# Two-layer hybrid decoder trunk: GpSimd takes 37 of the 258 weight-chunk subtractions, and the order of work is planned again

## The chip, the cores and the metric

The kernel runs on one core of one Trainium2 chip. A core has a TensorE (PE in the profile), a VectorE (DVE), a ScalarE (ACT), a GpSimd (POOL) and a SyncE (SP, which issues nearly all DMAs). The metric is the device time of one execution in microseconds. The kernel before takes 805.81 us, the median of three runs (805.7 to 805.99).

## The reference, cut to what matters

```python
for l in range(DEPTH):                       # 2 layers, x is 256 x 1024, float32
    h = rms_norm(x, g_mix[l])
    q_a, k_a, v_a, u_b, cq_c, ckv_c, kpe_c, gate_logits = split(h @ w_in[l])   # 1024 x 5280
    y_a = swa_attention(q_a, k_a, v_a, ...)        # 8 heads, window 128
    y_b = conformer_conv(u_b, w_dw[l], ...)        # GLU, depthwise conv of width 31, LayerNorm, swish
    y_c = mla_attention(cq_c, ckv_c, kpe_c, ...)   # low-rank query / key-value, 8 heads, causal
    branches = einsum([y_a, y_b, y_c], w_branch[l])
    x = x + (sigmoid(gate_logits) * branches).sum(branch) @ w_out[l]
    x = x + square(relu(rms_norm(x, g_mlp[l]) @ w_up[l])) @ w_down[l]   # 1024 -> 4096 -> 1024
return rms_norm(x, g_final)
```

Every weight is used once, and all is float32.

## The kernel before, in words

**Chunks.** The weights come through as 258 chunks of 128 x 1024 float32, 129 per layer, numbered i = 0 to 257 in the order of use: glu 8, kv 4, q 4, lr 2, up 3, gate 24, branch 12, out 8, mu 32 (the up projection of the MLP) and md 32 (its down projection). So layer 0 has kv0 as chunks 8 to 11, q0 as 12 to 15 and gate0 as 21 to 44; layer 1 has glu1 as 129 to 136, kv1 as 137 to 140, q1 as 141 to 144 and gate1 as 150 to 173.

**The split.** PE multiplies in a rounded 32-bit form (F32R). To keep float32's accuracy every chunk is split in two: `chunk()` loads it by DMA into a tile `raw` (5 buffers), ScalarE rounds it into `whi` (4 buffers), and VectorE subtracts, `wlo = raw - whi` (4 buffers). Each product is then three matmuls: high by high, high by low, low by high. `wlo` holds what the title of such a change calls the following bits. In the gate stage (`token_major`) a chunk is 12 matmuls of 512 columns, 4 of them with `wlo`.

**Other work of VectorE.** The depthwise convolution (`conv`) is 124 instructions per layer, each a multiply-add over 128 x 256 that reads `u` and `acc` in SBUF; it is spread between the splits of the kv, q and gate stages, and its result is needed at the last third of the branch stage. The softmax of both attentions, the evacuations of the accumulators in PSUM and the MLP's squares are VectorE's and ScalarE's too. GpSimd has 54 instructions: constants, a few statistics of two or four numbers a row, and one scaling of a 128 x 1024 tile (`gf`).

**The order of work.** Nothing is issued as the program is read. `Engine` records each operation with an estimated cost in a `Plan`; `Plan.place` then plays the whole program through as a list scheduler and writes the order of every engine's queue, which the chip follows as it stands. An operation's rank is the chunk number plus or minus an entry of the table `K`: `split_gate0` is how many chunks ahead gate0's splits rank, `conv_0` and `conv_end0` are where the convolution's first and last step rank. Among ready operations an engine takes the one that can start first, with a small allowance (`PATIENCE`) for a better-ranked one that comes a little later. `LATENCY` says how long after an operation on one engine its reader on another may start. So VectorE's queue is a fixed sequence: if one of its instructions is late, all behind it are.

All instructions carry one line of the helper that issues them (L407), so rows are told apart by tile names.

Of the kernel before, what the change touches and what calls it, by code (L numbers as in the profile page):

```python
# [16 lines left out]
ALU = mybir.AluOpType  # L17
# [40 lines left out]
for l in range(DEPTH):  # L58
# [2 lines left out]
    K.update({f"{s}{l}": v[l] for s, v in PLACE.items()})  # L61

K.update({
# [9 lines left out]
})  # L73

PATIENCE = {"PE": 0.0, "ACT": 0.001, "DVE": 0.006, "POOL": 0.0, "DMA": 0.0}

FLOOR = {"rope": 12.0, "dist": 20.0, "squares": 9.5}

# [126 lines left out]
class Op:  # L205
# [13 lines left out]
    "PE": {"PE": 0.0, "ACT": 0.2, "DVE": 0.2, "POOL": 0.2, "DMA": 0.2},  # L219
    "ACT": {"PE": 0.27, "ACT": 0.12, "DVE": 0.13, "POOL": 0.15, "DMA": 0.15},  # L220
    "DVE": {"PE": 0.25, "ACT": 0.13, "DVE": 0.13, "POOL": 0.16, "DMA": 0.15},
    "POOL": {"PE": 0.2, "ACT": 0.1, "DVE": 0.06, "POOL": 0.1, "DMA": 0.1},
    "DMA": {"PE": 2.3, "ACT": 2.3, "DVE": 2.3, "POOL": 2.3, "DMA": 2.3},
}

# [1 line left out]
class Plan:  # L227
# [68 lines left out]
    def place(self):  # L296
# [21 lines left out]
        while True:  # L318
            best = None
            for e, ops in avail.items():  # L320
                now, mine = clock[e], None
                for op in ops:
# [10 lines left out]
                    else:  # L333
                        c = (t + PATIENCE[e] * op.rank, op.rank, rank[op], t)
                        if mine is None or c < mine[0]:
# [144 lines left out]
def trunk(ctx: ExitStack, tc: tile.TileContext, A, out):  # L480
# [9 lines left out]
    T, V, SC = Engine(plan, "PE", nc.tensor), Engine(plan, "DVE", nc.vector), Engine(plan, "ACT", nc.scalar)  # L490
    G, Q = Engine(plan, "POOL", nc.gpsimd), Engine(plan, "DMA", nc.sync)
# [284 lines left out]
    used, section = [0], [""]  # L776
# [4 lines left out]
    def chunk(rotary=False):  # L781


        i = used[0]
        used[0] += 1
        with plan.at(i - 20.0):
            raw = plan.tile([P, 1024], F32, "raw")
            loads[i](raw)
        with plan.at(Key(i, **{"split_" + section[0]: -1}) if i else Key(-12)):
            hi, lo = plan.tile([P, 1024], F32R, "whi"), plan.tile([P, 1024], F32R, "wlo")  # L790
            cuts = () if rotary else ((0, 512), (512, 1024)) if i == 0 else ((0, 1024),)
            for c0, c1 in cuts:
                a, b, c = (v[:, c0:c1] for v in (raw, hi, lo))
                SC.copy(out=b, in_=a)
                V.tensor_tensor(out=c, in0=a, in1=b, op=ALU.subtract)
            if rotary:
                a, b, c = (v.rearrange("p (k c) -> p k c", c=256) for v in (raw, hi, lo))
                SC.copy(out=b[:, :, 0:192], in_=a[:, :, 0:192])
                V.tensor_tensor(out=c[:, :, 0:P], in0=a[:, :, 0:P], in1=b[:, :, 0:P], op=ALU.subtract)
                V.tensor_tensor(out=b[:, :, 192:256], in0=a[:, :, P:192], in1=b[:, :, P:192], op=ALU.subtract)  # L800
        plan.key = Key(i)
        return hi, lo
# [26 lines left out]
    def feature_major(xh, xl):  # L829

        banks = [bank("mm"), bank("mm")]
        for k in range(4):
            hi, lo = chunk()
            for ct in range(4):
                o = banks[ct // 2][:, (ct % 2) * 256:(ct % 2 + 1) * 256]
                for kk in range(2):
                    kt = 2 * k + kk
                    cs = slice(kk * 512 + ct * P, kk * 512 + (ct + 1) * P)
                    mm3(o, hi[:, cs], lo[:, cs], xh[kt // 4][:, kt % 4, :], xl[kt // 4][:, kt % 4, :],
                        kt == 0 and ct % 2 == 0, kt == 7 and ct % 2 == 1)  # L840
        return banks

    def feature_pairs(xp):


        banks = [bank(t) for t in ("mm", "mm", "ps", "ps")]
        for k in range(4):
            hi, lo = chunk()


            cts = [(ct,) for ct in range(4)] if k == 3 else [range(4)]
            for some in cts:
                for short in (False, True):
                    for ct in some:
                        for kk in range(2):
                            kt = 2 * k + kk
                            cs = slice(kk * 512 + ct * P, kk * 512 + (ct + 1) * P)
                            both = xp[kt // 4][:, kt % 4, :, :]
                            if short:
                                T.matmul(out=banks[ct][:, 0:S], lhsT=lo[:, cs], rhs=both[:, 0, :], start=False, stop=kt == 7)  # L860
                            else:
                                T.matmul(out=banks[ct], lhsT=hi[:, cs], rhs=both.rearrange("p a s -> p (a s)"), start=kt == 0,
                                         stop=False)
        return banks

    def token_major(banks, nchunk, kt0, ah, al, first, last):

        for k in range(nchunk):
            hi, lo = chunk()
            for t in range(2):  # L870
                for kk in range(2):
                    kt = kt0 + 2 * k + kk
                    ts = slice(t * P, (t + 1) * P)
                    cs = slice(kk * 512, (kk + 1) * 512)
                    mm3(banks[t], ah[kt // 4][:, kt % 4, ts], al[kt // 4][:, kt % 4, ts], hi[:, cs], lo[:, cs],
                        first and k == 0 and kk == 0, last and k == nchunk - 1 and kk == 1)
# [279 lines left out]
    for l in range(DEPTH):  # L1156
# [16 lines left out]
        for g in range(2):  # L1173
            bk = feature_major(xh, xl)
            with evacuation():
                gate, a = plan.tile([P, 512], F32, "p"), plan.tile([P, 512], F32, "pT")
# [255 lines left out]
```

## Time and profile before

| | |
|---|---|
| median of 3 runs | 805.81 us (805.7 to 805.99) |
| the profiled execution | 805.54 us, its span 803.8 us |
| PE busy | 789.3 us, 98% |
| DVE busy | 616.4 us, 77%, 982 instructions |
| ACT busy | 468.7 us, 58% |
| POOL busy | 23.9 us, 3%, 54 instructions |
| chain that ended last | PE 94% |

How to read it: busy is the time with an instruction in the engine; a matmul's end is modelled and overlaps the next, so the start-to-start distance of matmuls tells the pace. The last instruction of the program ends 803.8 us after the first; 1.7 us lie around that span. In the rows below a timeline row gives start, duration, engine, operation, output<-inputs with shapes, and in brackets the idle time of the engine before it with what ended it.

### The profile page before, as it was taken

How to read it: one execution, taken by the hardware profiler on the slowest of the kernel's cores; microseconds unless marked ns; L12 is line 12 of the kernel's file. 1: busy time of each engine (PE TensorE's matmuls, PEld its weight loads, DVE VectorE, ACT ScalarE, POOL GpSimd, SP SyncE). 2: the span in 40 equal slices, each digit the busy share in tenths (PEclk: the TensorE clock that was granted, in tenths of full speed). 3: DMA queues.
4: the chain of work that ended last, by engine and by line, in shares of the span. 5: the costliest groups of instructions: out<-in, count | busy, mean ns of one | idle time of the engine just before them, and what ended most of it. 6: DMA issues, size and time to landing. Idle time of an engine off the chain costs nothing.

```text
span 803.8 us, 12447 instructions
## 1 busy us (share of the span) xinstructions
PE 789.3 (98%) x4613; PEld 677.0 (84%) x4613; DVE 616.4 (77%) x982; ACT 468.7 (58%) x778; POOL 23.9 (3%) x54
## 2 busy tenths in 40 slices
PE   8999999999999999999999999999999999999996
PEld 6998888888888888888899978888888888888885
DVE  6999999979867887545469999888896778764543
ACT  7666875756555556435354599755646555653442
POOL 2200000000000000000000000000000000010000
PEclk9999999999999999999999999999999999999998
DMA  8697456534666665666667634366466666665641
GB/s 287 177 208 215 129 157 167 174 110 161 205 184 191 191 185 190 184 193 186 196 184 165 163 107 131 107 194 198 133 208 185 189 192 186 191 210 188 203 133 52
DMA packets 124044, 140.85 MB, mean 175 GB/s; under 512 B 51792, under 2 KB 68560, under 8 KB 123984
## 3 DMA queue, kind: packets, MB, share of 16 engines
q1 hardware_dynamic: 123280, 139.51, 59.0%
q8 instruction: 36, 0.59, 0.3%
q10 hardware_dynamic: 704, 0.56, 0.2%
q14 instruction: 24, 0.20, 0.1%
HBM read 138.93 MB, written 1.11 MB: 174 GB/s over the span
## 4 chain that ended last, share of the span: by engine, by line
PE 94%; ACT 1%; DVE 1%; DMA 1%; issue 1%; SPq 0%; POOL 0%; POOLq 0%; ACTq 0%; DVEq 0%
PE bank_mm L407 73%; PE bank_ps L407 17%; PE bank_yb L407 3%; PE bank_tp L407 1%; DMA raw<-in_w_in 1%; ACT p L407 1%; DVE wlo L407 0%; SPq L407 0%; ACT whi L407 0%; POOL rstd L407 0%; DVE rope L407 0%; ACT junk L407 0%; ACT x L407 0%; DVE kpe L407 0%; POOL s L407 0%
## 5 line engine op out<-in xcount | busy, mean ns | idle before, releaser
L407 DVE TENSOR_TENSOR wlo<-raw,whi 128x1024 fp32r<-128x1024 f32 (+1 forms) x259 | 313.4, 1212 | 146.9 <-ACT whi L407 144.9
L407 ACT CAST whi<-raw 128x1024 fp32r<-128x1024 f32 (+1 forms) x259 | 270.1, 1045 | 260.7 <-PE bank_mm L407 173.0
L407 PE MATMUL bank_mm<-xp,whi 128*128 128x256 f32 (+1 forms) x832 | 177.8, 320 | 0.4 <-DVE p L407 0.4
L407 PEld LDWEIGHTS bank_mm<-xp,whi 128*128 128x128 f32 x832 | 131.6, 191 | 5.3 <-PE bank_mm L407 0.6
L407 PE MATMUL bank_mm<-whi,xp 128*128 128x512 f32 x384 | 128.4, 400 | 0.2
L407 PE MATMUL bank_mm<-xp,wlo 128*128 128x256 f32 x528 | 120.3, 282 | 0.4 <-DVE wlo L407 0.4
L407 DVE SCALAR_TENSOR_TENSOR acc<-u,wdw,acc 128x256 f32<-128x256 f32 x240 | 101.8, 477 | 0.0
L407 PEld LDWEIGHTS bank_mm<-xp,wlo 128*128 128x128 f32 x528 | 93.6, 190 | 7.5 <-DVE wlo L407 0.8
L407 PE MATMUL bank_mm<-whi,fh 128*128 128x512 f32 x256 | 99.8, 390 | 0.0
L407 PE MATMUL bank_mm<-wlo,fh 128*128 128x512 f32 x256 | 99.6, 389 | 0.0
L407 PE MATMUL bank_mm<-whi,fl 128*128 128x512 f32 x256 | 99.6, 389 | 0.0
L407 PEld LDWEIGHTS bank_mm<-whi,xp 128*128 128x128 f32 x384 | 72.1, 188 | 17.0 <-issue 1.2
L407 PE MATMUL bank_mm<-wlo,xp 128*128 128x512 f32 x192 | 75.3, 392 | 2.1 <-DVE wlo L407 1.9
L407 PE MATMUL bank_ps<-xp,whi 128*128 128x512 f32 x256 | 71.9, 392 | 0.0
L407 PEld LDWEIGHTS bank_mm<-whi,fl 128*128 128x128 f32 x256 | 48.1, 188 | 9.9
L407 PEld LDWEIGHTS bank_mm<-wlo,fh 128*128 128x128 f32 x256 | 48.1, 188 | 9.9
L407 PEld LDWEIGHTS bank_mm<-whi,fh 128*128 128x128 f32 x256 | 48.1, 188 | 9.8
L407 PEld LDWEIGHTS bank_ps<-xp,whi 128*128 128x128 f32 x256 | 45.7, 188 | 7.9
L407 PEld LDWEIGHTS bank_mm<-wlo,xp 128*128 128x128 f32 x192 | 36.2, 188 | 9.5 <-DVE wlo L407 3.0
L407 PE MATMUL bank_ps<-xp,wlo 128*128 128x256 f32 x256 | 43.4, 282 | 0.0
L407 PEld LDWEIGHTS bank_ps<-xp,wlo 128*128 128x128 f32 x256 | 38.5, 191 | 2.8
L407 ACT ACTIVATE p<-p,rinv 128x128 f32<-128x128 f32 (+1 forms) x64 | 25.1, 453 | 1.5 <-DVE rinv L407 1.5
(214 smaller groups left out, 971.5 us busy)
## 6 DMA issues: line engine op xcount, KB each, us to landing
raw<-in_w_up SPq DMA_DIRECT2D x64, 512.0 KB, 3.9
raw<-in_w_down SPq DMA_DIRECT2D x64, 512.0 KB, 3.7
raw<-in_w_in SPq DMA_DIRECT2D x48, 512.0 KB, 3.6
raw<-in_w_in SPq DMA_DIRECT2D x48, 256.0 KB, 3.3
raw<-in_w_branch SPq DMA_DIRECT2D x24, 512.0 KB, 3.6
raw<-in_w_out SPq DMA_DIRECT2D x16, 512.0 KB, 4.0
raw<-in_w_in SPq DMA_DIRECT2D x32, 128.0 KB, 2.9
spread<-far SPq DMA_DIRECT2D x16, 128.0 KB, 3.8
```

Of the source, the lines that this page charges most:

```text
L407: return fn(**real)
```

## The change

In the seven stages named in a new table `SHARE`, a chunk whose number leaves the remainder 1 by 2 has its subtraction issued on GpSimd and not on VectorE. For the stages that are not in the table the divisor is 1 << 20, and chunk 1 (in glu0) leaves the remainder 1 by that as well. So it is 4 chunks of glu1 (129, 131, 133, 135), 2 each of kv0 (9, 11), kv1 (137, 139), q0 (13, 15) and q1 (141, 143), 12 each of gate0 (21 to 43) and gate1 (151 to 173), and chunk 1: 37 in all. Each is one `tensor_tensor` of 128 x 1024. The planner's latency from GpSimd to PE goes from 0.2 to 1.4, and the table `K`, and with it the order of all queues, is another one. `cost_pool`, which the planner uses, is as it was.

```diff
 K.update({
-    "bias": 3, "dist": -10, "small": 6, "rope": -23, "split_glu0": 21, "split_kv0": 17, "split_q0": 8, "split_lr0": -9,
-    "split_up0": 4, "split_gate0": 17, "split_branch0": -7, "split_out0": -41, "split_mu0": 10, "split_md0": 19,
+    "bias": -2, "dist": -5, "small": 6, "rope": -26, "split_glu0": 26, "split_kv0": -10, "split_q0": 16, "split_lr0": -6,
+    "split_up0": 24, "split_gate0": 23, "split_branch0": -13, "split_out0": -42, "split_mu0": 8, "split_md0": 18,
...
-    "conv_0": 41, "conv_end0": 55, "ln_0": 35, "split_glu1": 21, "split_kv1": 28, "split_q1": 20, "split_lr1": -15,
-    "split_up1": -21, "split_gate1": 23, "split_branch1": 10, "split_out1": -15, "split_mu1": -11, "split_md1": 24,
+    "conv_0": 28, "conv_end0": 91, "ln_0": 35, "split_glu1": 44, "split_kv1": 41, "split_q1": 28, "split_lr1": -17,
+    "split_up1": -5, "split_gate1": 27, "split_branch1": 18, "split_out1": 2, "split_mu1": -13, "split_md1": 9,
...
-    "conv_1": 24, "conv_end1": 150, "ln_1": 10,
+    "conv_1": 40, "conv_end1": 117, "ln_1": 2,
 })
 
 PATIENCE = {"PE": 0.0, "ACT": 0.001, "DVE": 0.006, "POOL": 0.0, "DMA": 0.0}
+
+SHARE = {"glu1": 2, "kv0": 2, "kv1": 2, "q0": 2, "q1": 2, "gate0": 2, "gate1": 2}
...
-    "POOL": {"PE": 0.2, "ACT": 0.1, "DVE": 0.06, "POOL": 0.1, "DMA": 0.1},
+    "POOL": {"PE": 1.4, "ACT": 0.1, "DVE": 0.06, "POOL": 0.1, "DMA": 0.1},
...
                 SC.copy(out=b, in_=a)
-                V.tensor_tensor(out=c, in0=a, in1=b, op=ALU.subtract)
+
+                (G if i % SHARE.get(section[0], 1 << 20) == 1 else V).tensor_tensor(out=c, in0=a, in1=b, op=ALU.subtract)
```

## Rows read from the trace of the kernel before

**Rows 1.** The page: busy time by engine, and the granted clock in 40 slices.
```profile
PE 789.3 (98%) x4613; PEld 677.0 (84%) x4613; DVE 616.4 (77%) x982; ACT 468.7 (58%) x778; POOL 23.9 (3%) x54
PEclk9999999999999999999999999999999999999998
```

**Rows 2.** Who waited for whom: us in total, times, longest.
```profile
ACT whi L407 <- PE bank_mm L407: 173.0, 113, 2.6
...
PE bank_mm L407 <- DVE wlo L407: 2.4, 4, 1.2
```

**Rows 3.** Timeline of PE where it waits for a low part.
```profile
73.20 0.50 PE L407 MATMUL bank_mm<-wlo,xp 128*128 128x512 f32 x1 [0.76 <-DVE wlo L407]
...
463.24 0.50 PE L407 MATMUL bank_mm<-wlo,xp 128*128 128x512 f32 x1 [1.18 <-DVE wlo L407]
```

**Rows 4.** Busy time by stretch: length, then PE, PEld, DVE, ACT, POOL, clock, DMA.
```profile
66.00:92.00 26.00, 25.13 (x191) 21.69 (x188) 25.33 (x64) 22.68 (x64) 1.77 (x4) 1.00 0.55 170
...
104.00:168.00 64.00, 64.00 (x344) 51.98 (x342) 61.83 (x120) 42.62 (x77) 0.00 (x0) 1.00 0.56 167
...
401.00:420.00 19.00, 19.00 (x139) 17.99 (x138) 11.49 (x16) 10.20 (x17) 1.49 (x5) 1.00 0.59 178
420.00:449.00 29.00, 29.00 (x245) 29.00 (x244) 27.67 (x50) 13.14 (x18) 0.00 (x0) 1.00 0.82 172
...
490.00:519.00 29.00, 29.00 (x187) 22.94 (x186) 25.84 (x57) 26.41 (x68) 0.00 (x0) 1.00 0.43 120
519.00:568.00 49.00, 49.00 (x223) 40.67 (x222) 40.91 (x65) 24.80 (x27) 0.69 (x1) 1.00 0.61 183
```

**Rows 5.** Timeline of ACT, DVE and PE around chunk 37 of gate0.
```profile
129.77 1.06 ACT L407 CAST whi<-raw 128x1024 fp32r<-128x1024 f32 x1 [1.08 <-PE bank_mm L407]
...
130.87 1.22 DVE L407 TENSOR_TENSOR wlo<-raw,whi 128x1024 fp32r<-128x1024 f32 x1
132.00 1.67 DVE L407 SCALAR_TENSOR_TENSOR acc<-u,wdw,acc 128x256 f32<-128x256 f32 x4
133.59 1.22 DVE L407 TENSOR_TENSOR wlo<-raw,whi 128x1024 fp32r<-128x1024 f32 x1
...
129.12 0.39 PE L407 MATMUL bank_mm<-wlo,xp 128*128 128x512 f32 x1
...
129.80 0.39 PE L407 MATMUL bank_mm<-wlo,xp 128*128 128x512 f32 x1
...
130.48 0.39 PE L407 MATMUL bank_mm<-wlo,xp 128*128 128x512 f32 x1
```

**Rows 6.** Busy time by stretch, the convolution's steps (tile acc) on DVE alone.
```profile
104.00:168.00 64.00, 37.21 (x89) 1.00 0.56 167
```

**Rows 7.** Timeline of POOL, then of DVE, from 17 to 22 us.
```profile
17.86 1.26 POOL L407 TENSOR_SCALAR rs<-rstd 128x2 f32<-128x2 f32 x1
...
17.82 1.23 DVE L407 TENSOR_TENSOR wlo<-raw,whi 128x1024 fp32r<-128x1024 f32 x1
...
19.90 1.99 POOL L407 TENSOR_TENSOR diff<-posb,posc 128x256 int32<-128x256 int32 x2 [0.77 <-DMA posc<-in_positions]
...
19.79 1.23 DVE L407 TENSOR_TENSOR wlo<-raw,whi 128x1024 fp32r<-128x1024 f32 x1 [0.74 <-ACT whi L407]
20.93 0.70 DVE L407 CAST rope<-posb 128x256 f32<-128x256 int32 x1
```

**Rows 8.** Groups of POOL instructions: busy us, mean ns, idle before.
```profile
L407 POOL TENSOR_TENSOR diff<-posb,posc 128x256 int32<-128x256 int32 x1 | 1.6, 1587 | 0.8 <-DMA posc<-in_positions 0.8
L407 POOL TENSOR_SCALAR s<-s 128x2 f32<-128x2 f32 x8 | 1.5, 191 | 113.0 <-DVE s L407 58.6 <-DVE den L407 53.9
```

**Rows 9.** Timeline of POOL and DVE from 709 to 713 us.
```profile
709.55 2.79 POOL L407 TENSOR_SCALAR gf<-gf 128x1024 f32<-128x1024 f32 x1 [86.81 <-DVE rel L407]
...
710.15 1.52 DVE L407 TENSOR_TENSOR wlo<-raw,whi 128x1024 fp32r<-128x1024 f32 x1 [0.40 <-ACT whi L407]
...
711.59 0.68 DVE L407 TENSOR_TENSOR fl<-rel,fh 128x512 fp32r<-128x512 f32 x1
```

8 rows, old and new, of the table K are left out of this document.

## The prediction

> **What bounds the kernel now.** I read the page first. TensorE is busy for 98% of the span and its clock is granted in full until the last slice [rows 1]. So time can be won only where TensorE waits, and can be lost wherever a weight chunk comes late. The list of waits says how little there is to win: TensorE's matmuls wait for a low part four times, 2.4 us in all [rows 2], and nearly all of that is two places, the first gate chunk of each layer, 0.76 us at 73 us and 1.18 us at 463 us [rows 3]. Next I asked for busy times by stretch. In the gate stage of layer 0 (104 to 168 us) VectorE is busy for 61.83 of 64 us; in the kv and q stages of layer 1 for 27.67 of 29; in the gate stage of layer 1 it has room, 3.2 us in 490 to 519 and 8.1 in 519 to 568; in glu1 7.5 of 19 [rows 4]. TensorE runs without a gap beside all four, so VectorE is full there but not late.
>
> How far it is from being late is seen at one chunk [rows 5]. With four buffers a chunk's high part starts when the chunk four places ahead has been used: ScalarE's rounding waits for TensorE 113 times [rows 2]. TensorE's last low-part matmul of chunk 33 is at 129.12, the rounding of chunk 37 starts at 129.77, its subtraction at 130.87 and ends at 132.09, 2.97 us after 129.12. The low-part matmuls of a gate chunk are 0.68 us apart (129.80, 130.48), so a chunk is 4 x 0.68 = 2.72 us. The first use of chunk 37 can't come before 129.12 + 0.68 + 3 x 2.72 = 137.96, that is 8.84 after. So a low part is 8.84 - 2.97 = 5.9 us ahead of its use when TensorE does nothing else. That is the cover under which the change works.
>
> **The change part by part.** Removed from VectorE: 37 subtractions. One takes VectorE 1.13 us from its start to the start of the next instruction (130.87 to 132.00) [rows 5], so 42 us over the kernel. Added to GpSimd: 37 two-input instructions of 128 x 1024, which this trace does not hold. Their price has to be bounded, and there are two: how long GpSimd takes, and what VectorE loses meanwhile.
>
> That the two engines stand in each other's way is plain in the rows. A 2-number scaling on GpSimd takes 0.19 us [rows 8]; the one at 17.86, started beside a subtraction of VectorE (17.82 to 19.05), took 1.26 and ended at 19.12, 0.07 after it [rows 7]. Five more small GpSimd instructions, not shown, end the same way behind a subtraction. So a VectorE instruction with two SBUF inputs shuts GpSimd out. The other direction has two rows. `gf`, one input of 128 x 1024, starts at 709.55; the subtraction that starts inside it, at 710.15, takes 1.52 instead of 1.23, 0.29 more, and so was let go at 710.44, 0.89 after `gf` began [rows 9]. And `diff`, two inputs of 128 x 256, was shut out until 21.02, ended at 19.90 + 1.59 = 21.49, and VectorE's cast that had started at 20.93 ended only at 21.63 [rows 7, 8]. I read this as a port that one of the two has at a time. `gf` then held it for 0.89 us with one input; two inputs of the same size make 1.78. `diff` gives 0.47 for a quarter of the size, so 1.88. The low end is that VectorE loses no more than the 0.29 seen. I take 1.78, because it is worked out from a row of the same width, and keep 0.29 and 1.88 for the range.
>
> The Trainium skill, "SBUF — State Buffer", section "Who interferes with whom", says that a VectorE instruction with two SBUF inputs and a GpSimd instruction that reads SBUF exclude each other for the whole instruction, whichever started first. The rows agree for GpSimd behind VectorE (1.26 us instead of 0.19), and for VectorE behind GpSimd as far as 0.29 us shows it. The skill's "GPSIMD Engine Reference", section 3.1, has 4497 ns for a two-input instruction of 2048 numbers a row; half of it, 2.25 us, is an estimate for one here. With 2.25 for 1.78 the sum below would be 4.2 us more.
>
> *Gate stage of layer 0.* The planner does not know of the port. It sees room on VectorE and fills it with steps of the convolution, each 0.397 us (four from 132.00 to 133.59) [rows 5]. In the 5.44 us of two chunks there is now one subtraction and room for (5.44 - 1.13) / 0.397 = 10 steps. On the chip these take 1.13 + 3.97 = 5.10 us, and GpSimd's subtraction holds the port for another 1.78, since both kinds of VectorE work have two SBUF inputs. That is 6.88 us for 5.44: VectorE falls behind by 1.44 us with each pair. 89 steps of the convolution lie in 104 to 168 us [rows 6], so about 9 pairs: 13.0 us. The lead of 5.9 us absorbs its part, and the 2.2 us that VectorE is idle there now [rows 4] another. TensorE waits for what is left: 13.0 - 5.9 - 2.2 = +4.9 us. Behind a late subtraction stand the convolution's steps and the next subtractions of VectorE, and TensorE waits for these. With a hold of 1.88 and no idle time to use it is 9 x 1.54 - 5.9 = +8.0; with 0.29 VectorE isn't late at all and it is 0.
>
> *Gate stage of layer 1.* 12 subtractions cost VectorE 12 x (1.78 - 1.13) = 7.8 us net, and it has 3.2 + 8.1 = 11.3 us idle [rows 4]. I cost it at nothing; the idle time hides it. If the planner packs the convolution there as in layer 0, some 6 pairs make 6 x 1.44 - 5.9 = +2.7.
>
> *glu1, kv1, q1.* In glu1 four holds of 1.78 (7.1 us) fit the 7.5 us of idle time [rows 4]; nothing. In kv1 and q1 four more cost a net 2.6 us, under the 5.9 us lead; nothing.
>
> *kv0, q0 and the first gate chunks.* Chunk 21, for which TensorE waits now [rows 3], goes to GpSimd, and between 66 and 92 us VectorE is busy for 25.33 of 26 us with softmax [rows 4]. Taking the subtraction away can end the waits, -2.4 us; a softmax step caught behind GpSimd twice costs 2 x 1.78 = +3.6. `split_gate0` ranks the chunk 6 places sooner than now, which speaks for a gain, the longer instruction against it. I take 0.
>
> *Chunk 1* moves too, in the first 12 us. It would be later by 1.78 - 1.13 = 0.65 us at least; I cost it at nothing, since VectorE's work there is mostly out of PSUM; 0.65 if the cover is not there.
>
> *Lateness of GpSimd's own results.* A subtraction there is done 1.78 us after a wait of up to 1.23 for VectorE, 1.8 us later than now at worst; the lead of 5.9 hides it. Statistics behind it in GpSimd's queue wait under 2 us, and none is near a subtraction that TensorE needs at once.
>
> Sum: 805.54 for the profiled execution (span 803.8 and 1.74 around it) + 4.9 = 810.4. The median of the runs is 0.27 above that execution, so 810.7 us.
>
> **The rivals.** *VectorE hardly loses anything (faster).* GpSimd takes the port only in VectorE's pauses, or gives it back after each 0.29 us or so. Then VectorE has 42 us more, the convolution ends sooner, and the waits for low parts at 73 and 463 us go: 805.8 - 2.4 = 803.4 us, at best 802 if the new order also closes small gaps elsewhere. For it speaks that 0.29 is all that a VectorE subtraction was ever seen to lose, and that GpSimd's `gf` took 2.79 us, as if it had been the one to yield [rows 9]; against it the cast held until 21.63 [rows 7]. It decides if the hold is under 5.44 - 5.10 = 0.34 us.
>
> *It cancels (no change).* The hold is real, but the lead and the idle time take it up: at 1.44 x 9 = 13.0 against 8.1 this needs a hold of about 1.2 us, or fewer convolution steps between the splits. Then 805.8, with small gains and losses of a microsecond.
>
> *GpSimd is starved (much slower).* If VectorE's back-to-back instructions keep the port, GpSimd's result is late until VectorE runs dry, and VectorE runs dry only when TensorE has stopped and no buffer comes free. Then no lead absorbs anything, and each of 9 pairs costs the full 1.78: +16 us, 821.8. `gf` ending only at 712.34, 0.07 after the second VectorE instruction behind it (711.59 + 0.68) [rows 9], speaks for it; that small instructions end right behind one subtraction, against.
>
> **How the numbers follow.** A measurement of this kernel can tell 0.2%, 1.6 us, from no change. Chances: the forecast 0.42, hardly any loss 0.30, cancelling 0.18, starved 0.10. Faster: 0.30 + 0.01 from the cancelling case = 0.31. Slower: 0.42 + 0.10 less 0.02 of the forecast's lower edge = 0.50. Same: 0.19. The forecast's own range is 807.5 (half of 4.9 lost) to 820 (8.0 + 2.7 + 3.6 = 14.3). The range that should hold 8 in 10 goes from 802 to 819: it takes in the gain of the first rival down to its best and leaves out the starved case, a little of the forecast's upper end and gains beyond 802.
>
> **What would show it.** Right: VectorE's subtractions and convolution steps that last 2 to 3 us beside GpSimd's; TensorE waiting for VectorE's (even) low parts between 115 and 165 us, some 5 us in all; the gate stage of layer 1 without such waits. Wrong: durations on VectorE unchanged at 1.23 and 0.48 beside GpSimd (then the first rival), or TensorE waiting for GpSimd's low parts, which last 5 us and more (then the starved one). The forecast fails too if the convolution is no longer packed into the gate stage.

## The result, and the profile after: 4.6% slower

The changed kernel takes 842.94 us (median of five runs, 842.64 to 843.31) against 805.70 (805.38 to 805.99) for the kernel before. The ratio is 1.0463, with a 95% interval of 1.0448 to 1.0479: 37 us slower, where the forecast said 5. The profiled execution takes 843.14 us, its span 841.4.

The page of the changed kernel: busy time by engine, the granted clock in 40 slices, and the chain that ended last, by engine.

```profile
PE 804.0 (96%) x4613; PEld 687.3 (82%) x4613; DVE 623.5 (74%) x945; ACT 467.7 (56%) x778; POOL 119.3 (14%) x91
...
PEclk9989999899999999999999999999999999999999
...
PE 73%; DVE 18%; ACT 4%; issue 3%; DMA 1%; POOL 0%; SPq 0%; POOLq 0%; DVEq 0%; ACTq 0%
```

Against [rows 1], VectorE has 37 instructions fewer and is busy for 7 us *more*. The chain that ended last was 94% TensorE before; now 18% of it is VectorE. The clock shows an 8 in two early slices. GpSimd, which got the work, has no share of the chain.

Two groups of instructions (count, busy us and mean ns of one, idle time before) show where the saving went.

```profile
L409 POOL TENSOR_TENSOR wlo<-raw,whi 128x1024 fp32r<-128x1024 f32 x37 | 94.8, 2561 | 388.0 <-ACT whi L409 350.2 <-DVE nm L409 31.3 <-DMA raw<-in_w_in 4.1
...
L409 DVE SCALAR_TENSOR_TENSOR acc<-u,wdw,acc 128x256 f32<-128x256 f32 x240 | 138.9, 635 | 0.0
```

The convolution's step lasts 635 ns on average; the same group of the kernel before has 477. That is 240 x 158 ns = 38 us lost, of 42 saved; the rest of the growth is spread over smaller groups. The timeline of VectorE, GpSimd and TensorE in the gate stage of layer 0 shows how it is lost, and what follows.

```profile
122.05 6.41 DVE L409 SCALAR_TENSOR_TENSOR acc<-u,wdw,acc 128x256 f32<-128x256 f32 x5
...
140.12 7.08 DVE L409 SCALAR_TENSOR_TENSOR acc<-u,wdw,acc 128x256 f32<-128x256 f32 x7
147.12 1.21 DVE L409 TENSOR_TENSOR wlo<-raw,whi 128x1024 fp32r<-128x1024 f32 x1
...
122.04 4.95 POOL L409 TENSOR_TENSOR wlo<-raw,whi 128x1024 fp32r<-128x1024 f32 x2 [7.65 <-ACT whi L409]
...
139.98 2.47 POOL L409 TENSOR_TENSOR wlo<-raw,whi 128x1024 fp32r<-128x1024 f32 x1
144.10 2.42 POOL L409 TENSOR_TENSOR wlo<-raw,whi 128x1024 fp32r<-128x1024 f32 x1 [1.65 <-ACT whi L409]
...
143.09 0.48 PE L409 MATMUL bank_mm<-whi,xp 128*128 128x512 f32 x1
148.39 0.80 PE L409 MATMUL bank_mm<-wlo,xp 128*128 128x512 f32 x1 [4.81 <-DVE wlo L409]
...
149.83 0.63 PE L409 MATMUL bank_mm<-wlo,xp 128*128 128x512 f32 x1
...
151.11 0.63 PE L409 MATMUL bank_mm<-wlo,xp 128*128 128x512 f32 x1
...
153.30 0.39 PE L409 MATMUL bank_mm<-wlo,xp 128*128 128x512 f32 x1
...
153.98 0.39 PE L409 MATMUL bank_mm<-wlo,xp 128*128 128x512 f32 x1
```

Beside two subtractions of GpSimd, which take 4.95 us, five convolution steps take 6.41 us; four take 1.67 in [rows 5], so five 2.07. The 4.34 us more are 2.17 for each subtraction. From 140.12 it happens twice again, VectorE's next low part ends only at 148.33, and TensorE stands for 4.81 us. After that, TensorE is slow as well: its low-part matmuls are 1.28 us apart (149.83, 151.11) and then again 0.68 (153.30, 153.98). The windows of that stretch (length, then PE, PEld, DVE, ACT, POOL, granted clock, DMA) give the level.

```profile
143.50:148.40 4.90, 0.09 (x2) 0.01 (x1) 4.90 (x7) 2.10 (x6) 2.42 (x1) 0.76 0.00 0
148.40:152.70 4.30, 4.30 (x10) 3.44 (x11) 4.30 (x11) 0.00 (x0) 0.00 (x0) 0.50 0.75 239
152.70:157.00 4.30, 4.30 (x20) 3.49 (x20) 4.30 (x12) 1.08 (x3) 0.00 (x0) 0.98 0.57 171
```

The clock falls to 0.50 of 2.4 GHz, 1.2 GHz, during TensorE's wait, and the first 4.3 us of work after it are 10 matmuls where the next 4.3 us are 20. So this wait is paid once while it lasts and a second time behind it. In the trace of before the clock is 1.00 beside the whole gate stage [rows 4].

What TensorE's matmuls waited for, over the whole kernel (us in total, times, longest):

```profile
PE bank_mm L409 <- DVE wlo L409: 6.3, 4, 4.8
PE bank_ps L409 <- DVE pairs L409: 5.2, 1, 5.2
PE bank_mm L409 <- DVE kT L409: 5.2, 1, 5.2
PE bank_ps L409 <- DVE p L409: 3.5, 2, 2.3
PE bank_mm L409 <- ACT cw L409: 2.7, 1, 2.7
PE bank_ps L409 <- ACT p L409: 1.4, 1, 1.4
PE bank_mm L409 <- DVE pT L409: 1.1, 1, 1.1
```

In [rows 2] low parts were the largest entry of this list, with 2.4 us. Now three quarters of it is something else: `kT` and `cw` empty the banks of the key-value product, VectorE's `p` is a step of the softmax that empties a bank, its `pT` empties a bank of glu1, and `pairs` holds the convolution's finished sums. Two of the places in the timeline:

```profile
44.82 4.94 DVE L409 SCALAR_TENSOR_TENSOR acc<-u,wdw,acc 128x256 f32<-128x256 f32 x7
49.68 1.21 DVE L409 TENSOR_TENSOR wlo<-raw,whi 128x1024 fp32r<-128x1024 f32 x1
50.81 0.41 DVE L409 TENSOR_TENSOR kT<-bank_mm,rb 128x256 f32<-128x256 f32 x1
...
45.78 0.28 PE L409 MATMUL bank_mm<-xp,wlo 128*128 128x256 f32 x1
51.28 0.80 PE L409 MATMUL bank_mm<-xp,whi 128*128 128x256 f32 x2 [5.21 <-DVE kT L409]
...
554.61 7.93 DVE L409 SCALAR_TENSOR_TENSOR acc<-u,wdw,acc 128x256 f32<-128x256 f32 x9
562.46 1.22 DVE L409 TENSOR_TENSOR wlo<-raw,whi 128x1024 fp32r<-128x1024 f32 x1
...
565.29 0.69 DVE L409 TENSOR_TENSOR pairs<-acc 128x512 f32<-128x512 f32 x1
...
566.03 1.22 PE L409 MATMUL bank_ps<-pairs,part 128*128 128x256 f32 x2 [5.23 <-DVE pairs L409]
```

After 45.78 TensorE has weights, but `kT` takes the result out of the bank that it wants next, and `kT` stands in VectorE's queue behind seven convolution steps and a split, 2 us late by a GpSimd subtraction and late already. At 560.8 it is the end of the convolution itself.

### The profile page after: what moved, and what is told of

Read it like the earlier page. It is cut to its first block, busy times and chain, and to the rows that moved or that the text cites. A ratio compares the mean times of both kernels' runs of the same rounds, so it can differ in the third digit from the quotient of the medians.

```text
span 841.4 us, 12455 instructions
## 1 busy us (share of the span) xinstructions
PE 804.0 (96%) x4613; PEld 687.3 (82%) x4613; DVE 623.5 (74%) x945; ACT 467.7 (56%) x778; POOL 119.3 (14%) x91
## 4 chain that ended last, share of the span: by engine, by line
PE 73%; DVE 18%; ACT 4%; issue 3%; DMA 1%; POOL 0%; SPq 0%; POOLq 0%; DVEq 0%; ACTq 0%
PE bank_mm L409 56%; PE bank_ps L409 13%; DVE acc L409 11%; DVE wlo L409 3%; PE bank_yb L409 2%; ACT p L409 2%; DVE nmc L409 1%; DMA raw<-in_w_in 1%; PE bank_tp L409 1%; ACT whi L409 1%; DVE p L409 0%; DVE rope L409 0%; ACT junk L409 0%; SPq L409 0%; DVE kTc L409 0%
## 5 line engine op out<-in xcount | busy, mean ns | idle before, releaser
L409 DVE TENSOR_TENSOR wlo<-raw,whi 128x1024 fp32r<-128x1024 f32 (+1 forms) x222 | 269.5, 1216 | 157.4 <-ACT whi L409 156.4
L409 PE MATMUL bank_mm<-xp,whi 128*128 128x256 f32 (+1 forms) x832 | 181.1, 324 | 9.1 <-DVE kT L409 5.2
L409 POOL TENSOR_TENSOR wlo<-raw,whi 128x1024 fp32r<-128x1024 f32 x37 | 94.8, 2561 | 388.0 <-ACT whi L409 350.2
L409 PEld LDWEIGHTS bank_mm<-xp,whi 128*128 128x128 f32 x832 | 134.3, 195 | 14.5 <-DVE kT L409 5.4
L409 DVE SCALAR_TENSOR_TENSOR acc<-u,wdw,acc 128x256 f32<-128x256 f32 x240 | 138.9, 635 | 0.0
L409 PE MATMUL bank_mm<-whi,xp 128*128 128x512 f32 x384 | 130.8, 408 | 0.1
L409 PE MATMUL bank_mm<-xp,wlo 128*128 128x256 f32 x528 | 122.0, 285 | 0.3 <-DVE wlo L409 0.2
L409 PEld LDWEIGHTS bank_mm<-whi,xp 128*128 128x128 f32 x384 | 74.4, 194 | 17.1 <-issue 1.0
L409 PE MATMUL bank_mm<-wlo,xp 128*128 128x512 f32 x192 | 77.2, 402 | 6.1 <-DVE wlo L409 6.1
```

Of the source, the lines that this page charges most:

```text
L409: return fn(**real)
```

## The experiments

All are given with median, ratio to the kernel before and its 95% interval. Three theories were tried: *port* (a GpSimd instruction that reads SBUF holds VectorE up), *order* (the new places, with splits and convolution packed otherwise, are slow by themselves) and *late results* (TensorE waits for what GpSimd makes).

**1. The old places, only the share on GpSimd.**

```diff
 # kernel before: K and LATENCY as they were
+SHARE = {"glu1": 2, "kv0": 2, "kv1": 2, "q0": 2, "q1": 2, "gate0": 2, "gate1": 2}
-                V.tensor_tensor(out=c, in0=a, in1=b, op=ALU.subtract)
+                (G if i % SHARE.get(section[0], 1 << 20) == 1 else V).tensor_tensor(out=c, in0=a, in1=b, op=ALU.subtract)
```

> The kernel before with one edit: the same 37 subtractions go to GpSimd, but with the old table of places and the old latency of 0.2. Theory P (the port: each of GpSimd's two-input subtractions keeps VectorE's two-SBUF-input instructions off the port for about 2.15 us, VectorE's fixed queue runs late, TensorE waits, and its clock falls after the long waits): a loss of the same kind, 825 to 850 us, since the planner here knows of the port as little as there. Theory O (the new order of work is what costs): near before, 803 to 809. Theory L (GpSimd's results simply come too late for TensorE): 815 to 850, with TensorE waiting for GpSimd's low parts.

847.79 us, 1.0525 (1.0509 to 1.0541). The time fits the ranges of *port* and of *late results*, but none of the waits of TensorE's matmuls is for a low part of GpSimd's, which *late results* asked for. The loss does not come with the places; with GpSimd's share the new ones are 5 us better than the old.

**2. The new places, all subtractions on VectorE.**

```diff
-                (G if i % SHARE.get(section[0], 1 << 20) == 1 else V).tensor_tensor(out=c, in0=a, in1=b, op=ALU.subtract)
+                V.tensor_tensor(out=c, in0=a, in1=b, op=ALU.subtract)
```

> The changed kernel with its new table of places and its latency, but every subtraction on VectorE; the queues are planned for that. Theory P: 803 to 810 us. Theory O: 830 to 845. Theory L: 803 to 810.

810.17 us, 1.0057 (1.0042 to 1.0072). The places alone cost 4.8 us (against 805.39 for the kernel before in the same round of runs), just above the range of the port theory. The timeline of TensorE has one long wait, ahead of the first attention, and the granted clock is 0.50 from 72 to 82 us, behind it:

```profile
71.76 1.87 PE L409 MATMUL bank_ps<-kT,qTa 64*128 64x256 f32 x6 [2.99 <-DVE p L409]
```

**3. The changed kernel's order, its 37 subtractions carried out by VectorE.** The planner still takes them for GpSimd's, so they stand in the same places.

```diff
+    GV = Engine(plan, "POOL", nc.vector)
-                (G if i % SHARE.get(section[0], 1 << 20) == 1 else V).tensor_tensor(out=c, in0=a, in1=b, op=ALU.subtract)
+                (GV if i % SHARE.get(section[0], 1 << 20) == 1 else V).tensor_tensor(out=c, in0=a, in1=b, op=ALU.subtract)
```

> The order of the changed kernel, planned as if GpSimd did the 37 subtractions, but they are issued to VectorE's queue at that place. VectorE then spends 1.13 us on each where it lost 2.15 to the port. Theory P: a smaller loss, 810 to 825 us: in the gate stage a pair of chunks takes 5.10 + 1.13 = 6.23 us of VectorE for 5.44, 0.8 late per pair and not 1.8. Theory O: 838 to 845, as the order is the same. Theory L: 803 to 810, since the low parts are made in 1.2 us and not 2.4.

821.22 us, 1.0191 (1.0174 to 1.0208). An engine that does 42 us of work which its plan did not hold is 11 us late at the end, and still 22 us better off than with GpSimd's "help". This is inside the range of the port theory and outside the other two.

**4. The same order, GpSimd writes and reads nothing.**

```diff
-                (G if i % SHARE.get(section[0], 1 << 20) == 1 else V).tensor_tensor(out=c, in0=a, in1=b, op=ALU.subtract)
+                if i % SHARE.get(section[0], 1 << 20) == 1:
+                    plan.add("POOL", lambda c=c: [nc.gpsimd.memset(c.real().bitcast(F32), 0.0) for _ in range(4)],
+                             Engine.cost_pool("tensor_tensor", {"out": c}) * MARGIN["POOL"], [a, b], [c])
...
```

> The order of the changed kernel in every queue, but in place of each of the 37 subtractions GpSimd writes zeros into the tile four times over (the low parts of these chunks are left out): about as long on GpSimd, 2.5 to 4 us, and it reads nothing. Theory P: VectorE's durations stay at 0.48 and 1.22 and the loss is gone, 802 to 808 us. Theory O: 838 to 845. Theory L: about as late as GpSimd's subtraction, so 830 to 845.

809.93 us, 1.0053 (1.0038 to 1.0068). Groups, then TensorE's two largest waits, then the same five steps that took 6.41:

```profile
L799 POOL MEMSET wlo<- 128x1024 f32 x148 | 141.8, 959 | 304.5 <-PE bank_mm L409 276.7 <-PE bank_ps L409 21.4
...
L409 DVE SCALAR_TENSOR_TENSOR acc<-u,wdw,acc 128x256 f32<-128x256 f32 x240 | 100.3, 479 | 0.0
```

```profile
PE bank_ps L409 <- DVE p L409: 2.3, 1, 2.3
PE bank_mm L409 <- DVE wlo L409: 1.0, 2, 0.8
```

```profile
122.21 2.06 DVE L409 SCALAR_TENSOR_TENSOR acc<-u,wdw,acc 128x256 f32<-128x256 f32 x5
```

This decides it. GpSimd is busier than in the changed kernel (141.8 against 94.8 us), and TensorE, VectorE and ScalarE work in the same order. But VectorE keeps its pace, and 33 of the 37 us are gone. What is left, 2 us above the range of the port theory, is about what experiment 2 has with another order by the same places. The writes wait for a free buffer and not for the rounding, so the results come about as late as the changed kernel's (on average 2.4 us after the end of the chunk's rounding, 2.6 there), not later; against *late results* experiment 5 is the clearer one.

**5. The same order, one input.**

```diff
...
+                    plan.add("POOL", lambda b=b, c=c: nc.gpsimd.tensor_scalar(out=c.real(), in0=b.real(), scalar1=0.0, scalar2=None, op0=ALU.mult),
+                             Engine.cost_pool("tensor_tensor", {"out": c}) * MARGIN["POOL"], [a, b], [c])
...
```

> The order of the changed kernel, but each of the 37 subtractions on GpSimd is a multiplication of the high part by zero: one input of 128 x 1024 and not two (the low parts of these chunks are left out). Theory P: a one-input instruction holds the port for about 0.89 us, so the convolution's steps beside it take about 1.3 us and not 2.6, and the time lies between that with no hold (809.9) and that with 2.15 (842.9): by a straight line 824, by the lead that absorbs the first part 812 to 820. If the conflict belongs to two-input instructions alone: 808 to 811.

811.88 us, 1.0079 (1.0062 to 1.0096): between the two ranges, just under what the port theory had and just over that of a conflict of two-input instructions alone. The time does not tell them apart; the rows do. The convolution's group, then one of the held steps and the GpSimd instruction beside it:

```profile
L409 DVE SCALAR_TENSOR_TENSOR acc<-u,wdw,acc 128x256 f32<-128x256 f32 x240 | 112.6, 526 | 0.0
```

```profile
120.29 1.25 DVE L409 SCALAR_TENSOR_TENSOR acc<-u,wdw,acc 128x256 f32<-128x256 f32 x1
...
116.15 6.86 POOL L799 TENSOR_SCALAR wlo<-whi 128x1024 fp32r<-128x1024 f32 x1 [2.13 <-ACT whi L409]
```

A step loses 0.77 us (1.25 for 0.48, not 2.17), and here GpSimd is the one that waits, 6.86 us for an instruction that takes 3.01 on average. So one input conflicts too, but that is nearly free: 2 us in all. GpSimd's results come 3.1 us after the end of the chunk's rounding on average, later than the changed kernel's 2.6, and cost next to nothing: *late results* is out.

**6 and 7. The planner told of the hold**, with the new places (6) and with the old (7).

```diff
+PORT = 2.15
...
+            op.port = engine == "POOL" and cost > 2.0 and len(reads) == 2
...
+            if op.port:
+                clock["DVE"] = max(clock["DVE"], t) + PORT
```

> The changed kernel, and the planner keeps VectorE free for 2.15 us from the start of each of GpSimd's subtractions. Theory P with the queue's order as the reason for the size of the loss (the planner packs the convolution into time that the port takes away): most of the loss goes, 808 to 818 us, since VectorE's total work grows only by 37 x (2.15 - 1.13). If it is the lost VectorE time itself, whatever the order: 830 to 843.

> The same rule in the planner, with the old table of places and the old latency of 0.2 from GpSimd to TensorE. Theory P: 804 to 815 us, under the run with the new places, which alone cost 4.8. If the lost VectorE time counts whatever the order: 835 to 848, as with the old places before (847.8).

853.99 us, 1.0598 (1.0583 to 1.0614), and 844.68, 1.0487 (1.0466 to 1.0509). What was expected of an order at fault (808 to 818, 804 to 815) fell in both. 844.68 is inside the range for VectorE's lost time (835 to 848); 853.99 is above both of its ranges. In 6, TensorE's waits changed their names and did not shrink; these two alone make 25.3 us, as much as the whole list of the changed kernel above:

```profile
PE bank_mm L414 <- ACT yb_h L414: 13.0, 2, 6.5
PE bank_ps L414 <- DVE pairs L414: 12.3, 3, 5.5
```

The window of the convolution's steps alone, 104 to 168 and 168 to 200 us:

```profile
104.00:168.00 64.00, 32.16 (x63) 0.00 (x0) 1.00 0.53 164
168.00:200.00 32.00, 12.43 (x28) 1.06 (x1) 1.00 0.48 157
```

The planner leaves VectorE free where GpSimd reads, so 63 steps of the convolution lie in the gate stage instead of the 89 of the kernel before [rows 6]. The rest come in the branch stage, and `yb_h`, which is made from the convolution, is late there. So it is not only that the planner did not know: in the gate stage of layer 0 VectorE has no 2 us to give for each subtraction. The rule asks for more than the port takes, though: it keeps back all of VectorE's work, also the steps out of PSUM, which experiment 10 shows unheld. A planner that told the two apart was not tried.

**8 to 10. The share by stages**: only kv and q (8), only the gates (9), only glu1 (10). Chunk 1 goes to GpSimd in each.

```diff
-SHARE = {"glu1": 2, "kv0": 2, "kv1": 2, "q0": 2, "q1": 2, "gate0": 2, "gate1": 2}
+SHARE = {"kv0": 2, "kv1": 2, "q0": 2, "q1": 2}    # 8: nine subtractions
+SHARE = {"gate0": 2, "gate1": 2}                  # 9: twenty-five
+SHARE = {"glu1": 2}                               # 10: five
```

> The changed kernel with only the kv and q stages in SHARE (8 subtractions, and chunk 1): gates and glu1 on VectorE, planned for that. Theory P: 8 holds of 2.15 in stages where VectorE is full. In the changed kernel the chunks of q0 and q1 end 5.7 and 5.5 us later by the port and the half clock behind the waits, on top of some 4.8 of the new places: 814 to 824 us. If the gates are where it is lost, as the prediction had it: 809 to 812.

> The changed kernel with only the two gate stages in SHARE (24 subtractions, and chunk 1). The run with the kv and q stages alone was 18.1 us over the run with the new places alone. Theory P, stages add up: 842.9 - 18.1 = 825, so 820 to 830 us. If the gate stages are covered by the 5.9 us lead of their splits: 810 to 815, and what the kv and q stages do goes up when the gates follow. If the gates carry the loss, as the prediction had it: over 830.

> The changed kernel with only glu1 in SHARE (4 subtractions, and chunk 1), where VectorE is idle for two fifths of the time. Theory P: the holds fall into idle time and the time stays that of the new places alone, 809 to 812 us. If any subtraction on GpSimd costs its share of the loss: 810.2 + 4 x 0.9 = 814.

828.28 us, 1.0279 (1.0264 to 1.0294); 838.09, 1.04 (1.0386 to 1.0414); 811.37, 1.0066 (1.0052 to 1.0080). Against the new places alone (810.17) that is +18.1 for nine, +27.9 for 25, and +1.2 for five, whose interval overlaps that of the places alone. The sum of the parts, 47, is more than the 33 of the whole; each plan has its own order, so parts can't be added. Experiment 8 is above both ranges that were named for it. Experiment 9 is above the 820 to 830 of the port theory and in the range for gates that carry the loss; but with +18.1 from kv and q, they do not carry it alone. Experiment 10 is where the port theory had it. TensorE's largest waits, kv and q first, then the gates:

```profile
PE bank_mm L409 <- DVE kT L409: 5.2, 1, 5.2
PE bank_mm L409 <- DVE gate L409: 2.9, 2, 2.1
PE bank_mm L409 <- ACT cw L409: 2.7, 1, 2.7
```

```profile
PE bank_mm L409 <- DVE wlo L409: 7.4, 6, 4.8
PE bank_ps L409 <- DVE pairs L409: 6.6, 1, 6.6
PE bank_tp L409 <- ACT pT L409: 4.9, 2, 4.7
```

With kv and q alone the low parts are not among the three: all three are for banks to be emptied. One of the subtractions of glu1 in experiment 10, with nothing beside it on VectorE but two residual steps of 0.75 us that read PSUM:

```profile
408.66 2.40 POOL L409 TENSOR_TENSOR wlo<-raw,whi 128x1024 fp32r<-128x1024 f32 x1 [3.05 <-ACT whi L409]
```

**11. The same order, each GpSimd subtraction in four pieces of 256 columns.**

```diff
...
+                    def pieces(a=a, b=b, c=c):
+                        ra, rb, rc = a.real(), b.real(), c.real()
+                        for n in range(0, 1024, 256):
+                            nc.gpsimd.tensor_tensor(out=rc[:, n:n + 256], in0=ra[:, n:n + 256], in1=rb[:, n:n + 256], op=ALU.subtract)
...
```

> The order of the changed kernel, but each of GpSimd's 37 subtractions is issued as four of 256 numbers a row, so that VectorE gets the port between them. Theory P, the lost VectorE time counts: the holds are four times as many and a quarter as long, and the time stays at 835 to 848 us. If it is the length of a single hold, which catches a short softmax step or an evacuation for 2 us: 815 to 830.

832.16 us, 1.0333 (1.0317 to 1.0349), between the two expectations. Groups:

```profile
L409 DVE TENSOR_TENSOR wlo<-raw,whi 128x1024 fp32r<-128x1024 f32 x216 | 268.0, 1243 | 157.5 <-ACT whi L409 156.3 <-DMA relb<-in_rel_bias 0.4
L409 DVE SCALAR_TENSOR_TENSOR acc<-u,wdw,acc 128x256 f32<-128x256 f32 x240 | 134.5, 617 | 0.0
```

VectorE loses nearly as much as in the changed kernel: 240 x (617 - 479) + 216 x (1243 - 1224) ns = 37 us on these two groups against experiment 4, where the changed kernel loses 39. Yet 11 us are won, and the wait for `kT` is 3.7 us instead of 5.2. That speaks for the length of one hold as a cost beside the sum of all; no run varies the length alone.

**12. A try at a faster kernel**: the kernel before, nothing on GpSimd, with the splits of the first gate chunks, for which TensorE waits in [rows 3], cut into halves.

```diff
-            cuts = () if rotary else ((0, 512), (512, 1024)) if i == 0 else ((0, 1024),)
+            cuts = () if rotary else ((0, 512), (512, 1024)) if i in (0, 21, 150) else ((0, 1024),)
```

> The kernel before, nothing on GpSimd, with the first gate chunk of each layer (21 and 150) rounded and subtracted in two halves of 512, as chunk 0 is: what TensorE waits for at these two places is the 1.05 + 1.22 us from the start of the rounding to the end of the subtraction. If that wait is all there is to win, each is shorter by up to 1 us and the kernel takes 803.5 to 805; if the order of the softmax steps behind it gets worse, 805.4 to 809.

807.74 us, 1.0022 (1.0014 to 1.0031): no gain, and in the range named for a worse order of the softmax. The waits for low parts sink from 2.4 to 1.7 us, and a wait of 1.6 us for `pT` is there instead. No version beat the kernel before.

## Why the prediction was wrong, point by point

The profiled executions of before, after and experiment 4 can be set side by side, since in after and 4 TensorE, VectorE and ScalarE do the same work in the same order, and only what GpSimd does for the 37 chunks differs. Each cell is how much later than in the kernel before TensorE's last matmul with that chunk starts, counted in the order of the matmuls; the port's part is the growth of after less that of 4.

| up to the end of | after | experiment 4 | port's part | forecast |
|---|---|---|---|---|
| chunk 20: all up to gate0, and attention's start | +7.1 | -2.1 | 9.2 | 0 |
| chunk 48: gate0, first third of branch0 | +21.0 | +3.0 | 8.8 | +4.9 |
| chunk 128: rest of layer 0 | +21.1 | +3.1 | 0 | 0 |
| chunk 144: glu1, kv1, q1 | +26.6 | +2.9 | 5.7 | 0 |
| chunk 177: up to gate1, first third of branch1 | +38.1 | +5.6 | 8.8 | 0 |
| chunk 257: rest of layer 1 | +38.1 | +5.6 | 0 | 0 |

- *"a port that one of the two has at a time"*: right for two inputs, and shown by experiment 4. *"I take 1.78"*: too little; it is 2.17, above the upper bound of 1.88. Both came from rows in which GpSimd was held up itself, or had one input. The Trainium skill, "SBUF — State Buffer", section "Who interferes with whom", has the two exclude each other for the whole instruction, and lets a GpSimd instruction that only writes go free; the runs agree with both (2.17 of the 2.40 us that one takes alone; 479 ns beside the writes), but not for GpSimd instructions with one input, where 0.77 us are lost at the step shown in experiment 5. The Trainium skill's "GPSIMD Engine Reference", section 3.1, with its 4497 ns for twice the size, gave the prediction's estimate of 2.25, nearer than 1.78. By that estimate the forecast would have been 814.9, still 28 us short: the price of the hold is not the step that failed.
- *Gate stage of layer 0, +4.9 us of waits for low parts*: the waits came as said. They are 6.3 us in all, 1.0 in experiment 4, so 5.3 from the port, and the long one is at 143 us, inside the stretch that was named. That 4.9 comes so close is in part luck: with the measured 2.17 the 1.44 us of each pair become 1.83, and the same sum gives 9 x 1.83 - 5.9 - 2.2 = 8.4. And the stage as a whole is 8.8 us later by the port, in part because the clock falls at that wait.
- *"That is the cover under which the change works"*: this is the step that failed. The 5.9 us are the lead of a split, and I applied them to VectorE as a whole. Behind a held instruction stand also `kT`, `pT`, `p` and `pairs`, and they have no such lead: the first three empty banks that TensorE's next matmuls go into, and `pairs` is an operand that TensorE uses as soon as it is there. kv1 and q1 were costed at nothing by that cover, kv0 and q0 by a balance of small gains and losses; the table has 5.7 us for kv1 and q1 with glu1, and 9.2 us for the stretch with kv0 and q0, where the one wait for `kT` is 5.2. The nine subtractions of experiment 8, in a plan of their own, are +18.1.
- *"the idle time hides it"* (gate1): the 11.3 us exist, but not where the holds fall. In the trace of before 8.0 of them are 19 short waits for ScalarE's roundings, and with the convolution ahead of `pairs` the sum of the holds reaches TensorE in one wait of 5.2 us.
- *glu1 nothing*: right (experiment 10); its subtractions lie beside VectorE's waits and its steps out of PSUM, and in the changed kernel TensorE is 18.0 us behind experiment 4 both at the start and at the end of glu1. *Chunk 1 nothing*: right; TensorE is at -0.7 us at the end of glu0.
- *The places*: not costed at all. Alone they are +4.8 us.
- *The clock*: not thought of. Six stretches of the changed kernel are at level 0.50 before its end. Five come with the waits for `kT`, `p`, the low part, `cw` and `pairs`; the sixth, from 497.6 us, comes in the attention, behind two waits of 0.25 and 0.53 us. In them the matmuls' starts are some 12.3 us further apart than the same forms have them at full clock. Experiment 4 has two such stretches, behind the same wait for `p` (2.3 us, so not the port's) and at the same place in the attention of layer 1; there it is 3.2.
- *GpSimd is starved*: no. Its 37 take 2.56 us on average, 2.40 alone, and none of TensorE's waits of 0.3 us or more is for one of them. That the loss is larger than that rival's 16 us has nothing to do with its reason. *VectorE hardly loses anything*: no. *It cancels*: no.

So the sum that I should have had, against the profiled execution of before (843.14 - 805.54 = 37.6): the places 5.1 (experiment 4's own profiled execution, 810.64); low parts 5.3; the other six waits of the list 19.1, less 2.7 in experiment 4, is 16.4; the clock 12.3 - 3.2 = 9.1. Together 35.9. The other 1.7 are smaller waits and the matmuls right behind a wait, which start some 0.16 us later than its idle time says. That the first is the order's and the rest the port's is shown by runs; how the rest divides between waits and clock is worked out from the traces, and no run separates them. Open is also whether some other order could bear GpSimd's share; two plans that knew the hold, with places that were not fitted to it, could not.

## What to carry to other kernels

When work goes from VectorE to GpSimd, look at what VectorE does meanwhile: if its instructions take two inputs from SBUF, a two-input instruction on GpSimd beside them is paid by VectorE in nearly its full length, here 2.17 us for 1.13 saved. It cost nothing only where VectorE stood idle or read PSUM, and even there nothing was won. A lead measured for one kind of work covers that kind alone: ask of everything that shares the queue, evacuations (the steps that empty a PSUM bank) and operands first, how soon its reader wants it. And a wait of TensorE can cost more than it lasts: here five of 2.3 to 5.2 us each came with some microseconds at half clock.

## What the runs showed of the hardware

- GpSimd and VectorE stand in each other's way by what is read, not by being busy: 142 us of GpSimd writes left the convolution's step at 479 ns, 37 one-input reads made it 526, 37 two-input reads 635.
- With one input the hold isn't the whole instruction: 0.77 us of VectorE's time at the step shown, while GpSimd's instruction was stretched to 6.86.
- VectorE's instructions with an operand in PSUM were not held where the traces show them beside a subtraction: in experiment 10, `pT` and `p` ran beside the one at 421.02 in 0.69 us each, as in the kernel before.
- In the changed kernel each of TensorE's five waits of 2.3 to 5.2 us came with a stretch at 1.2 GHz, and a sixth stretch came without such a wait; in the kernel before, whose longest wait is 1.2 us, the page shows no lower clock ahead of the last slice [rows 1].
